# Products of the conditioning vector with the modulations' weights: from VectorE multiply-adds to float32 matmuls in quarters of the TensorE array, and the first stage's weights loaded in rows of 2 KB

## The chip, the core and the metric

One NeuronCore of a Trainium2 chip runs the whole program. Its engines work through queues of their own, each in order: TensorE (PE: matmuls, float32 and a faster one-pass form called fp32r), VectorE (DVE), ScalarE (ACT), GpSimd (POOL) and SyncE (SP), which here issues nearly all DMAs. They meet through semaphores. The metric is the device time of one execution in microseconds; lower is better.

## The reference

One decoder block over 1024 tokens of 1024 channels. A conditioning vector `c` gives six modulation vectors of 1024 channels each; they shift, scale and gate what goes into and comes out of two sublayers. The change touches only how `mod` is computed, and how the weights of `u` (the first 512 columns of `w_in`) are loaded:

```python
cond = jax.nn.silu(c)
mod = (cond @ w_ada[l] + b_ada[l])[:, None, :]        # w_ada: 1024 x 6144
sh1, sc1, g1, sh2, sc2, g2 = jnp.split(mod, N_ADA, axis=-1)
h = modulate(rmsnorm(x, norm1_g[l]), sh1, sc1)        # x (1 + sc1) + sh1
proj = h @ w_in[l]
u, q, k, v, gate_a, gate_b = jnp.split(proj, IN_SPLITS, axis=-1)
y_a = s5_branch(u, ...) @ w_a[l]                      # a state-space scan, then a gated unit w_glu
y_b = stick_breaking_attention(q, k, v) @ w_b[l]
merged = (jax.nn.sigmoid(gate_a) * y_a + jax.nn.sigmoid(gate_b) * y_b) @ w_o[l]
x = x + g1 * merged                                    # then a feed-forward part with sh2, sc2, g2
```

All is float32.

## The kernel before

The code is Python that records instructions; a scheduler then orders them on each engine by a simulated timeline, within the data dependencies and the turns of the buffers, and tiles are handed out in the order in which the program asks for them. A tile whose buffer is still in use makes its first writer wait, and a pool that is closed gives its memory to the next pool, whose first writers wait for all that used it.

*The opening, `start` (from L507).* The 1024 x 1024 input is loaded in two halves of four row tiles; each half is normalised and transposed by TensorE into `xT`. The vector is held as `cond[p, k] = silu(c)[8p + k]`. For each of eight blocks of 128 channels, `ada(k)` loads the shift and the scale columns of `w_ada` into a tile `wa` (two DMAs in rows of 512 bytes, three buffers), VectorE forms `acc`, a sum over `k` of `wa[:, k] * cond[:, k]`, in one multiply (L555) and seven multiply-adds (L559), and a matmul with a column of ones (L563) adds up the 128 partitions. Then `modulate(k, 0)` writes the channels of the first half as two fp32r terms, high (ScalarE, L571) and low (VectorE L572, GpSimd L573), and `product` (L582) adds them into the four `u` results. The weights of `u` come in four blocks of 128 columns, all 1024 rows of each, in rows of 512 bytes, and are split into high and low as well. The second half of the input follows when five blocks are done.

*The S5 stage.* From the end of the opening the state-space branch (class `S5`) runs in four rounds: `tables(m)`, a long run of small GpSimd operations (L67 to L72), then `run(m)` with loads of `u`, TensorE products (L287, L325, L326) and VectorE scans. Between its parts TensorE works off the value projection (`v_proj`, L639) and the first eight gates (`gate`, L619); gates 6 and 7 may load their weights only after the last S5 product. The results of `v_proj` and of the gates take turns in two PSUM buffers, `mm` of the pools `mm` and `mg`.

*`ada_rest` (L753 to L765)* belongs to the same stage. It forms the other four modulation vectors, 4096 columns of `w_ada`, in eight pieces of 512 columns: four loads `aw` of two `k` each (512 KB, rows of 2 KB, two buffers), eight VectorE operations into `acc` (L762, L764), and a store to `aD` in DRAM. `aD` is read back much later, for the merge and the feed-forward part, where the 128 partitions are added up.

*After it, `glu` (from L801)* reads the S5 result back from DRAM (`raw`, L810), applies GELU (L811), splits it into `yp` and multiplies it with `w_glu` (TensorE, tiles `ga`). Its tiles lie in the memory that the S5 stage gives back. The query and key projections and the attention follow.

Of the kernel before, what the change touches and what calls it, by code (L numbers as in the profile page):

```python
# [9 lines left out]
F32 = mybir.dt.float32  # L10
# [327 lines left out]
AK = 2  # L338

GAB = 4  # L340
TPB, WAB = 2, 3
# [5 lines left out]
XH1 = 5  # L347
# [37 lines left out]
class Block:  # L385
# [121 lines left out]
    def start(self, const, up):  # L507
# [4 lines left out]
        w_v = i["w_ada"].rearrange("o (p k) (s n) -> (o p) k s n", k=KT, n=1024)  # L512
        self.hT = [[pool.tile([P, 2, 512], F32R, name=n) for _ in range(KT)] for pool, n in ((self.PA, "pa"), (self.PB, "pb"))]
        with self.pool("s0", 1, side="right") as sp, self.pool("s0a", 1, side="right") as ap, \
# [6 lines left out]
            ws, chain = [], []  # L521
# [26 lines left out]
            def ada(k):  # L548
                w = ap.tile([P, KT, 2, P], F32, name="wa", bufs=WAB)
                for q in range(2):  # L550
                    self.last_ada = nc.sync.dma_start(out=w[:, :, q], in_=w_v[:, :, q, P * k:P * k + P])
                if k < 4:
                    ws.append(self.u_weight(k, ring=None if k < 3 else (up, "u3h", "u3l", self.wring[0][3], "ws", 2)))
                acc = ap.tile([P, 2, P], F32, name="acc", bufs=2)
                ins = nc.vector.tensor_scalar(acc, w[:, 0], self.cond[:, 0:1], None, ALU.mult)  # L555
                if chain:
                    self.after(ins, chain[-1])
                for j in range(1, KT):
                    ins = nc.vector.scalar_tensor_tensor(acc, w[:, j], self.cond[:, j:j + 1], acc, ALU.mult, ALU.add)  # L559
                chain.append(ins)  # L560
                for q in range(2):
                    o = ps[:, q, k:k + 1]
                    nc.tensor.matmul(o, lhsT=acc[:, q], rhs=self.ones[:, 0:1], start=True, stop=True)  # L563
                b = self.cols[:, 64:80].rearrange("p (q k) -> p q k", q=2)
                nc.vector.tensor_tensor(mod[:, :, k], ps[:, :, k], b[:, :, k], ALU.add)
                nc.vector.scalar_tensor_tensor(G[:, k:k + 1], mod[:, 1, k:k + 1], 1.0, self.cols[:, 48 + k:49 + k], ALU.add, ALU.mult)
# [13 lines left out]
            def product(q, m, k, h):  # L580
                for n, (a, b) in enumerate(PRODUCTS):
                    nc.tensor.matmul(q, lhsT=ws[m][a][:, k], rhs=self.hT[h][k][:, b], start=k + n == 0, stop=k + n == KT + 1)  # L582
# [6 lines left out]
            for k in range(KT):  # L589
                ada(k)  # L590
                modulate(k, 0)
                for m in range(min(k + 1, 4)):
# [714 lines left out]
```

## Time and profile before

| what | us |
|---|---|
| median of 3 runs | 1623.77 |
| lowest and highest of them | 1619.41, 1629.88 |
| the profiled execution | 1618.39 |
| its span, first to last instruction | 1616.7 |
| TensorE busy | 1475.8 (91%) |
| VectorE busy | 1106.9 (68%) |
| GpSimd busy | 705.3 (44%) |
| ScalarE busy | 626.6 (39%) |

Busy times are unions over the span, so they say nothing of which engine ends last in a given stage. In rows of the profile `L559` is a line of the kernel, `out<-in` are the program's names of tiles, `x8` is a count, and a bracket holds the idle time ahead of a row with what ended it. Rows of the clock give the share of its full speed that TensorE was granted.

### The profile page before, as it was taken

What the parts mean: (1) busy time and instruction counts of PE and PEld (TensorE: products, weight loads), DVE (VectorE), ACT (ScalarE), POOL (GpSimd) and SP (SyncE); (2) the same over time, 40 slices, a digit from 0 to 9 for tenths busy, and PEclk for the clock granted to TensorE, in tenths of its full rate; (3) what the DMA queues carried; (4) which work ended last, traced back from release to release, by engine and by line L of the source; (5) the groups of instructions that cost most, each with busy time, mean ns of one, the idle gap of its engine ahead of it and who ended that gap; (6) DMA issues with size and microseconds to landing.
All of it is one profiled execution on the core that took longest, in us unless ns stands there. A gap on an engine that the chain in (4) does not pass through costs nothing.

```text
span 1616.7 us, 18487 instructions
## 1 busy us (share of the span) xinstructions
PE 1475.8 (91%) x6738; PEld 1153.8 (71%) x6738; DVE 1106.9 (68%) x1399; ACT 626.6 (39%) x816; POOL 705.3 (44%) x553
## 2 busy tenths in 40 slices
PE   4888897999989899999999979999999998999965
PEld 3688676787645476665778758888888886887854
DVE  6989887342475645545743788666566659999978
ACT  4421111532575745535423643332323334443313
POOL 3559784010110102110340454445555458788784
PEclk9999999899899999999999989999999999999988
DMA  9585665627101012111742323333333146445302
GB/s 241 164 205 171 167 184 159 181 85 221 46 0 40 27 46 85 53 46 46 242 175 91 109 74 111 98 99 113 114 114 117 65 155 249 147 159 163 98 26 104
DMA packets 191139, 193.55 MB, mean 120 GB/s; under 512 B 28069, under 2 KB 141833, under 8 KB 191049
## 3 DMA queue, kind: packets, MB, share of 16 engines
q1 hardware_dynamic: 179976, 184.38, 36.9%
q10 hardware_dynamic: 11072, 8.00, 1.7%
q8 instruction: 53, 0.87, 0.2%
q14 instruction: 38, 0.30, 0.1%
HBM read 142.40 MB, written 48.76 MB: 118 GB/s over the span
## 4 chain that ended last, share of the span: by engine, by line
PE 49%; DVE 21%; issue 9%; POOL 8%; DMA 8%; ACT 5%; SPq 1%; ACTq 0%; DVEq 0%; POOLq 0%
PE mm L619 11%; PE tq L1031 10%; PE wo L1031 8%; PE wo L912 5%; PE ga L619 3%; PE gu L1031 3%; PE z L699 2%; DVE acc L559 2%; PE mm L746 2%; DMA aw<-in_w_ada_dram 2%; PE acc L736 2%; PE acc L741 1%; DVE acc L764 1%; DVE x L1119 1%; POOL pb L1123 1%
## 5 line engine op out<-in xcount | busy, mean ns | idle before, releaser
L430 POOL TENSOR_TENSOR ws<-wb 128x1024 f32<-128x1024 f32 x29 | 73.2, 2526 | 102.9 <-DVE wl L433 59.5
L738 DVE TENSOR_TENSOR wa<-wa,acc 128x512 f32<-128x512 f32 (+3 forms) x96 | 52.9, 552 | 87.5 <-PE acc L736 87.0
L414 POOL TENSOR_TENSOR wl<-ws,wh 128x1024 fp32r<-128x1024 f32 x10 | 25.4, 2544 | 192.7 <-ACT wh L411 192.7
L413 POOL TENSOR_SCALAR wgh<-wgs 128x1024 fp32r<-128x1024 f32 x8 | 8.7, 1092 | 206.8 <-PE mm L619 146.1
L430 POOL TENSOR_TENSOR wgs<-wb 128x1024 f32<-128x1024 f32 x15 | 37.0, 2466 | 107.3 <-DVE x L433 36.1
L743 ACT ACTIVATE wa<-wa 128x1024 f32<-128x1024 f32 (+3 forms) x48 | 40.4, 842 | 67.8 <-DVE wa L738 67.6
L1084 POOL TENSOR_TENSOR pa<-pa,row 128x1024 f32<-128x1024 f32 x22 | 64.4, 2950 | 2.1 <-DMA pa<-in_w_ffn_down_dram 2.1
L714 DVE COPY wa<-z 128x1024 f32<-128x1024 f32 (+1 forms) x40 | 44.6, 1116 | 29.1 <-ACT ws L713 18.0
L619 PE MATMUL mm<-pa,wh 128*128 128x512 f32 x192 | 63.9, 410 | 0.0
L1022 POOL TENSOR_TENSOR f<-f,f 128x512 f32<-128x512 f32 x30 | 50.1, 1694 | 26.8 <-DVE f L1012 18.3
L619 PE MATMUL mm<-pb,wh 128*128 128x512 f32 x192 | 60.4, 395 | 0.8 <-DVE k L673 0.8
L717 DVE SCALAR_TENSOR_TENSOR ws<-wa,ws 128x1024 f32<-128x1024 f32 (+1 forms) x40 | 48.2, 1208 | 16.9 <-ACT ws L716 16.7
L619 PE MATMUL mm<-pa,wgh 128*128 128x512 f32 x176 | 56.5, 402 | 1.3 <-POOL wgh L413 0.9
L619 PE MATMUL mm<-pb,wgh 128*128 128x512 f32 x176 | 57.4, 406 | 0.2 <-ACT gst L656 0.2
L411 ACT CAST wh<-ws 128x1024 fp32r<-128x1024 f32 x30 | 31.4, 1046 | 63.8 <-PE wo L912 27.6
L764 DVE SCALAR_TENSOR_TENSOR acc<-aw,cond,acc 128x512 f32<-128x512 f32 x56 | 46.9, 837 | 12.2 <-DMA aw<-in_w_ada_dram 11.7
L719 DVE TENSOR_TENSOR wl<-ws,wh 128x1024 fp32r<-128x1024 f32 (+1 forms) x40 | 46.0, 1150 | 13.0 <-ACT wh L718 12.3
L699 PE MATMUL z<-q,k 64*128 64x512 f32 (+3 forms) x192 | 48.3, 574 | 4.8 <-DVE wa L714 2.9
L713 ACT ACTIVATE ws<-z 128x1024 f32<-128x1024 f32 (+1 forms) x40 | 37.4, 936 | 33.6 <-DVE wl L719 32.4
L718 ACT CAST wh<-ws 128x1024 fp32r<-128x1024 f32 (+1 forms) x40 | 38.3, 957 | 28.9 <-PE acc L741 22.5
L1011 ACT ACTIVATE f<-f 128x1024 f32<-128x1024 f32 x22 | 23.4, 1061 | 62.3 <-DVE f L1051 32.5
L1104 POOL TENSOR_TENSOR wb<-pa 128x512 f32<-128x512 f32 x23 | 40.6, 1775 | 15.7 <-DVE wxl L1102 5.5
(736 smaller groups left out, 4892.5 us busy)
## 6 DMA issues: line engine op xcount, KB each, us to landing
aw<-in_w_ada_dram SPq DMA_DIRECT2D x32, 512.0 KB, 5.2
hD<-f SPq DMA_DIRECT2D x30, 512.0 KB, 3.4
wb<-in_w_ffn_gate_dram SPq DMA_DIRECT2D x44, 256.0 KB, 4.0
wb<-in_w_ffn_up_dram SPq DMA_DIRECT2D x44, 256.0 KB, 4.5
pa<-in_w_ffn_down_dram SPq DMA_DIRECT2D x22, 512.0 KB, 6.3
wb<-hD SPq DMA_DIRECT2D x40, 256.0 KB, 2.8
ws<-in_w_in_dram SPq DMA_DIRECT2D x19, 512.0 KB, 6.5
x<-in_x_dram SPq DMA_DIRECT2D x16, 512.0 KB, 7.1
```

The source lines that it names most:

```text
L430: (add or nc.gpsimd).tensor_tensor(st, a, b, op)
L619: self.nc.tensor.matmul(ps, lhsT=w[a][:, k], rhs=act[h][k][:, b], start=(j == 0), stop=(j == n - 1))
L699: ins = nc.tensor.matmul(z[:, x, f:f + w], lhsT=k[h, P * kb:P * kb + P], rhs=q[h, 512 * Q + c:512 * Q + 512], start=f == 0, stop=not diag)
L714: nc.vector.tensor_copy(at, z)
L717: nc.vector.scalar_tensor_tensor(st, at, 0.0, st, ALU.max, ALU.add)
L719: nc.vector.tensor_tensor(lt, st, ht.bitcast(F32), ALU.subtract)
L738: nc.vector.tensor_tensor(a[:, x, f], a[:, x, f], acc[:, x, c], ALU.subtract)
L764: nc.vector.scalar_tensor_tensor(acc, w[:, j], cj, acc, ALU.mult, ALU.add)
L912: nc.tensor.matmul(ps, lhsT=mg[t // 4][k][:, a, P * (t % 4):P * (t % 4) + P], rhs=ws[k // 2][b][:, k % 2], start=(j == 0), stop=(j == 23))
L1022: nc.gpsimd.tensor_tensor(o, a, b, op)
L1031: self.nc.tensor.matmul(ps, lhsT=w[x][:, q, k], rhs=self.B[i](y, k), start=(j == 0), stop=(j == 11))
L1084: nc.gpsimd.tensor_tensor(w, w, g2, ALU.mult)
```

## The change

Both places form the products by TensorE. The vector is widened once to `cond32`, 32 equal columns of `cond[:, k] / 32` for each `k`. `ada_mm` multiplies a piece of 512 columns of `w_ada` with the 32 columns of one `k` and writes 32 PSUM partitions, the quarter `k % 4` of the array; `k` and `k + 4` add up in one quarter. The 128 partitions of the result then again sum to the wanted product, so what follows it is unchanged. The matmuls are plain float32. ScalarE copies the result into `acc`.

In the opening the eight steps become two groups of four channel blocks. Each loads shift and scale columns in four DMAs of 1 MB, in rows of 2 KB, into four buffers. The transposes and these results share the PSUM pool `tp` of two buffers. The weights of `u` now come in four blocks of two `k` and all 512 columns, in rows of 2 KB. The second half of the input is loaded behind group 1's loads.

In `ada_rest` the loads stay as they are, but the result takes one of the PSUM buffers `mm` that `v_proj` and the gates take their turns in.

```diff
 KT = 8
 MASKED = -1.0e30
 
-AK = 2
+AK, ARB = 2, 2
 
 GAB = 4
-TPB, WAB = 2, 3
+TPB, WAB = 2, 4
 GUB, WOB, TQB = 1, 3, 4
 ZPB = 2
 GB = 2
 WAB2, WSB, WHB = 4, 2, 2
 
-XH1 = 5
 QPIN = -10
 PINS = (0, 5, 10, 15, 20, 25, 30, 35)
 
...
         nc, i = self.nc, self.i
         ss = const.tile([P, KT], F32, name="ss1")
         x_v = i["x"].rearrange("o (t p) d -> p (o t) d", p=P)
-        w_v = i["w_ada"].rearrange("o (p k) (s n) -> (o p) k s n", k=KT, n=1024)
+        w_v = i["w_ada"].rearrange("o (p k) n -> (o p) k n", k=KT)
+        self.cond32 = up.tile([P, KT, 32], F32, name="cond32")
+        nc.vector.tensor_scalar(self.cond32, self.cond.unsqueeze(2).broadcast_to([P, KT, 32]), 1.0 / 32.0, None, ALU.mult)
         self.hT = [[pool.tile([P, 2, 512], F32R, name=n) for _ in range(KT)] for pool, n in ((self.PA, "pa"), (self.PB, "pb"))]
         with self.pool("s0", 1, side="right") as sp, self.pool("s0a", 1, side="right") as ap, \
                 self.pool("s0p", 1, PSUM) as pp, self.pool("s0t", TPB, PSUM) as tp, self.pool("s0m", 5 - TPB, PSUM) as mp:
...
             ps = pp.tile([P, 2, KT], F32, name="adap")
             mod = const.tile([P, 2, KT], F32, name="mod1")
             G = const.tile([P, KT], F32, name="G1")
-            ws, chain = [], []
+            ws = []
 
             def half(h):
                 r = self.rstd(const, ss[:, 4 * h:4 * h + 4], 4)
...
                     sq = xT[:, 2 * (t % 4):2 * (t % 4) + 2, 512:1024]
                     nc.scalar.activation(sq, x[t].rearrange("p (a b) -> p a b", a=2), AF.Square, accum_out=ss[:, t:t + 1])
 
-            def ada(k):
-                w = ap.tile([P, KT, 2, P], F32, name="wa", bufs=WAB)
+            def ada(g):
+
                 for q in range(2):
-                    self.last_ada = nc.sync.dma_start(out=w[:, :, q], in_=w_v[:, :, q, P * k:P * k + P])
-                if k < 4:
-                    ws.append(self.u_weight(k, ring=None if k < 3 else (up, "u3h", "u3l", self.wring[0][3], "ws", 2)))
-                acc = ap.tile([P, 2, P], F32, name="acc", bufs=2)
-                ins = nc.vector.tensor_scalar(acc, w[:, 0], self.cond[:, 0:1], None, ALU.mult)
-                if chain:
-                    self.after(ins, chain[-1])
-                for j in range(1, KT):
-                    ins = nc.vector.scalar_tensor_tensor(acc, w[:, j], self.cond[:, j:j + 1], acc, ALU.mult, ALU.add)
-                chain.append(ins)
-                for q in range(2):
-                    o = ps[:, q, k:k + 1]
-                    nc.tensor.matmul(o, lhsT=acc[:, q], rhs=self.ones[:, 0:1], start=True, stop=True)
+                    parts = []
+                    for a in range(2):
+                        w = ap.tile([P, 4, 512], F32, name="wa", bufs=WAB)
+                        n = 2 * q + g
+                        self.last_ada = nc.sync.dma_start(out=w, in_=w_v[:, 4 * a:4 * a + 4, 512 * n:512 * n + 512])
+                        parts.append(w)
+                    t = tp.tile([P, 512], F32, name="tp")
+                    for k in range(KT):
+                        self.ada_mm(t, k, parts[k // 4][:, k % 4])
+                    acc = ap.tile([P, 512], F32, name="acc", bufs=2)
+                    nc.scalar.copy(acc, t)
+                    for k in range(4):
+                        nc.tensor.matmul(ps[:, q, 4 * g + k:4 * g + k + 1], lhsT=acc[:, P * k:P * k + P], rhs=self.ones[:, 0:1], start=True, stop=True)
+                for a in (2 * g, 2 * g + 1):
+                    ws.append(self.u_weight(a, ring=None if a < 3 else (up, "u3h", "u3l", self.wring[0][3], "ws", 2)))
+                s = slice(4 * g, 4 * g + 4)
                 b = self.cols[:, 64:80].rearrange("p (q k) -> p q k", q=2)
-                nc.vector.tensor_tensor(mod[:, :, k], ps[:, :, k], b[:, :, k], ALU.add)
-                nc.vector.scalar_tensor_tensor(G[:, k:k + 1], mod[:, 1, k:k + 1], 1.0, self.cols[:, 48 + k:49 + k], ALU.add, ALU.mult)
+                nc.vector.tensor_tensor(mod[:, :, s], ps[:, :, s], b[:, :, s], ALU.add)
+                nc.vector.scalar_tensor_tensor(G[:, s], mod[:, 1, s], 1.0, self.cols[:, 48 + 4 * g:52 + 4 * g], ALU.add, ALU.mult)
 
             def modulate(k, h):
                 t = self.hT[h][k]
...
 
             def product(q, m, k, h):
                 for n, (a, b) in enumerate(PRODUCTS):
-                    nc.tensor.matmul(q, lhsT=ws[m][a][:, k], rhs=self.hT[h][k][:, b], start=k + n == 0, stop=k + n == KT + 1)
+                    nc.tensor.matmul(q, lhsT=ws[k // 2][a][:, k % 2, P * m:P * m + P], rhs=self.hT[h][k][:, b], start=k + n == 0, stop=k + n == KT + 1)
 
             def store(m, h, q):
                 u = up.tile([P, 8, 64], F32, name="us", bufs=3)
                 self.upin = nc.scalar.copy(u, q.rearrange("p (c j) -> p j c", j=8))
                 nc.sync.dma_start(out=self.uD[P * m:P * m + P, :, 64 * h:64 * h + 64], in_=u)
 
-            for k in range(KT):
-                ada(k)
-                modulate(k, 0)
-                for m in range(min(k + 1, 4)):
-                    for kk in range(k if m < k else 0, k + 1):
-                        product(acc[m], m, kk, 0)
-                if k == XH1:
+            for g in range(2):
+                ada(g)
+                if g:
                     load(1)
+                for k in range(4 * g, 4 * g + 4):
+                    modulate(k, 0)
+                    for m in range(4):
+                        product(acc[m], m, k, 0)
             for m in range(4):
                 store(m, 0, acc[m])
             half(1)
...
     def w3(self, w, n=P):
         return [t.rearrange("p (k n) -> p k n", n=n) for t in w]
 
-    def u_weight(self, m, ring=None):
-        return self.w3(self.weight(self.in_cols(P * m), lo_eng=self.nc.gpsimd, ring=ring))
+    def u_weight(self, a, ring=None):
+        src = self.i["w_in"][0].rearrange("(k p) n -> p k n", p=P)[:, 2 * a:2 * a + 2, 0:512]
+        return self.w3(self.weight(src, lo_eng=self.nc.gpsimd, ring=ring), 512)
 
     def v_proj(self, vp):
 
...
             self.split(hi[:, s], lo[:, s], av)
 
 
+    def ada_mm(self, ps, k, w):
+
+        q = slice(32 * (k % 4), 32 * (k % 4) + 32)
+        self.nc.tensor.matmul(ps[q], lhsT=self.cond32[:, k], rhs=w, start=k < 4, stop=k >= 4)
+
     def ada_rest(self, ap, first):
         nc, i = self.nc, self.i
         w_v = i["w_ada"].rearrange("o (p k) n -> (o p) k n", k=KT)
         for n in range(4, 12):
+            ws = []
+            for k in range(0, KT, AK):
+                w = ap.tile([P, AK, 512], F32, name="aw", bufs=ARB)
+                self.after(nc.sync.dma_start(out=w, in_=w_v[:, k:k + AK, 512 * n:512 * n + 512]), first)
+                ws.append(w)
+            ps = self.mm.tile([P, 512], F32, name="mm")
+            for k in range(KT):
+                self.ada_mm(ps, k, ws[k // AK][:, k % AK])
             acc = ap.tile([P, 512], F32, name="acc", bufs=2)
-            for k in range(0, KT, AK):
-                w = ap.tile([P, AK, 512], F32, name="aw", bufs=2)
-                self.after(nc.sync.dma_start(out=w, in_=w_v[:, k:k + AK, 512 * n:512 * n + 512]), first)
-                for j in range(AK):
-                    cj = self.cond[:, k + j:k + j + 1]
-                    if k + j == 0:
-                        nc.vector.tensor_scalar(acc, w[:, j], cj, None, ALU.mult)
-                    else:
-                        nc.vector.scalar_tensor_tensor(acc, w[:, j], cj, acc, ALU.mult, ALU.add)
+            nc.scalar.copy(acc, ps)
             nc.sync.dma_start(out=self.aD[:, n - 4], in_=acc)
 
     def ada_row(self, row, n, tp, pp, tags):
```

The order of the instructions changes with it. First, the opening, on VectorE before (the `wa` multiplies, then the modulation's scale `G` and the scaled input `xT`):

```order
L555 TENSOR_SCALAR acc<-wa,cond 128x256
L559 SCALAR_TENSOR_TENSOR acc<-wa,cond,acc 128x256 x7
L555 TENSOR_SCALAR acc<-wa,cond 128x256
L559 SCALAR_TENSOR_TENSOR acc<-wa,cond,acc 128x256 x3
L565 TENSOR_TENSOR mod_151<-adap,cols 128x2
L559 SCALAR_TENSOR_TENSOR acc<-wa,cond,acc 128x256
L566 SCALAR_TENSOR_TENSOR G_152<-mod_151,cols 128x1
L559 SCALAR_TENSOR_TENSOR acc<-wa,cond,acc 128x256 x2
L572 TENSOR_SCALAR xT<-xT,G_152,mod_151 128x512
```

and on TensorE after (`tp` are transposes and then the new products, `cond_118` is `cond32`, `adap` the sums over partitions, `mm` the `u` products):

```order
L537 MATMUL tp<-ident,x 128x128 x32
L759 MATMUL tp<-wa,cond_118 32x512 x16
L564 MATMUL adap<-ones,acc 128x1 x8
L586 MATMUL mm<-pa,wh 128x512 x4
L759 MATMUL tp<-wa,cond_118 32x512 x8
L586 MATMUL mm<-pa,wh 128x512
L586 MATMUL mm<-pa,wl 128x512
```

The multiply-adds of a block stood between the modulations of the blocks before it; now two sets of eight matmuls stand ahead of the first modulation and a third in the midst of the first products.

Second, the queue of SP at the end of the S5 stage, before (`tz`, `u` and `yD` are S5's, `gD` the gates' stores, `raw` the first loads of `glu`):

```order
L758 DMA aw<-in_w_ada_dram 128x2x512
L657 DMA gD<-gst 128x512 x2
L758 DMA aw<-in_w_ada_dram 128x2x512
L270 DMA tz<-rt 16x8x112
L270 DMA tz<-rt 16x8x80
L270 DMA tz<-rt 16x8x48
L270 DMA tz<-rt 16x8x16
L758 DMA aw<-in_w_ada_dram 128x2x512
L657 DMA gD<-gst 128x512
L765 DMA aD<-acc 128x512
L657 DMA gD<-gst 128x512
L404 DMA ws<-in_w_in_dram 128x8x128
```

and after, from the last gate's store to the first load of `glu`:

```order
L662 DMA gD<-gst 128x512 x2
L768 DMA aw<-in_w_ada_dram 128x2x512 x2
L403 DMA wgs<-in_w_a_dram 128x4x256
L768 DMA aw<-in_w_ada_dram 128x2x512 x2
L775 DMA aD<-acc 128x512
```

Six more pieces follow in the same way, four `aw` loads and one `aD` store at a time, up to this end of the stretch on SP:

```order
L775 DMA aD<-acc 128x512
L768 DMA aw<-in_w_ada_dram 128x2x512 x2
L775 DMA aD<-acc 128x512
L820 DMA raw<-yD 128x512 x8
L403 DMA ws<-in_w_a_dram 128x4x256
```

Before, the last `aw` load stood ahead of gate 6's weights, between S5's own transfers. Now two `aw` loads are issued near the start of the stage and the other 30 stand behind the last gate's store and ahead of all loads of `raw`.

Third, TensorE from the last gate (`mm<-pb,wgh`) to the first product of `glu` (`ga<-yp`), before:

```order
L619 MATMUL mm<-pb,wgh 128x512 x2
L619 MATMUL mm<-pb,wgl 128x512
L619 MATMUL mm<-pb,wgh 128x512 x2
L619 MATMUL mm<-pb,wgl 128x512
L619 MATMUL ga<-yp,wh 128x512 x2
L619 MATMUL ga<-yp,wl 128x512
L619 MATMUL ga<-yp,wh 128x512 x2
```

and after:

```order
L623 MATMUL mm<-pb,wgh 128x512 x2
L623 MATMUL mm<-pb,wgl 128x512
L623 MATMUL mm<-pb,wgh 128x512 x2
L623 MATMUL mm<-pb,wgl 128x512
L759 MATMUL mm<-aw,cond_118 32x512 x64
L623 MATMUL ga<-yp,wh 128x512 x5
L623 MATMUL ga<-yp,wl 128x512
```

Nothing stood between them before; now all 64 products of `ada_rest` do.

## The prediction

> **What bounds the kernel now.** I read the page's totals first, then stretches of time, then the chain of waits inside the two stages that the change touches, then single tiles. The totals say only that TensorE is the busiest engine. The stretches say where it is not the bound (columns: stretch, its length, busy time and instructions of each engine, granted TensorE clock, DMA share, GB/s):
>
> ```profile
> span 1616.7 us, 18487 instructions
> ...
> 15.30:81.00 65.70, 52.57 (x211) 38.24 (x210) 61.25 (x103) 30.10 (x47) 33.71 (x21) 0.95 0.73 196
> ...
> 98.50:311.50 213.00, 184.90 (x1130) 160.67 (x1130) 163.65 (x262) 42.62 (x62) 141.50 (x266) 0.93 0.64 179
> 311.50:337.50 26.00, 23.95 (x99) 19.29 (x98) 15.35 (x19) 18.48 (x25) 2.39 (x1) 0.93 0.32 106
> 337.50:403.00 65.50, 65.31 (x289) 53.75 (x287) 19.15 (x25) 16.14 (x24) 3.21 (x4) 1.00 0.55 169
> ```
>
> From 15.3 to 81 us VectorE is busy for 61.25 of 65.7 us: the opening is bound there. From 98.5 to 311.5 us run the S5 branch, the value projection, eight gates and, on VectorE, the rest of the modulations (`ada_rest`). TensorE is busy for 184.9 of 213 us, VectorE 163.7, GpSimd 141.5. From 337.5 on TensorE has no gap, so a shift of that point is kept. The chain of waits for the opening, and for 98 to 312 us, by line:
>
> ```profile
> by line: DVE acc L559 43.7%; DVE xT L572 10.9%; DMA x<-in_x_dram 7.9%; DMA wa<-in_w_ada_dram 6.7%; DVE acc L555 5.0%; issue 4.6%; DVE G L566 3.3%; DVE x L532 2.8%; PE mm L582 2.1%; ACT pa L571 2.0%; POOL pa L573 1.6%; SPq L542 1.6%; DVE rv
> ```
>
> ```profile
> by line: DMA aw<-in_w_ada_dram 11.9%; DVE acc L764 9.0%; issue 7.1%; DMA u<-uD 5.8%; DVE scr L303 4.4%; DMA raw<-yD 3.5%; DMA ws<-in_w_in_dram 3.0%; POOL scr L71 2.8%; POOL scr L70 2.8%; DVE scr L310 2.7%; POOL p L67 2.6%; POOL p L68 2.6%;
> ```
>
> So the chain puts 48.7% of 81 us (39 us) on the opening's multiply-adds, and 20.9% of 214 us (45 us) on `ada_rest`'s multiply-adds and loads. That is what the change removes or moves. The second stage however is a mesh, not one chain; TensorE's own waits there were for
>
> ```profile
> PE s5a L235 <- POOL scr L71: 9.8, 4, 3.7
> PE mm L639 <- DVE vst L643: 7.3, 4, 2.8
> PE s5a L326 <- DVE h L318: 5.8, 2, 5.4
> PE s5a L325 <- DMA tz<-rt: 3.6, 1, 3.6
> PE s5a L235 <- POOL scr L72: 1.6, 1, 1.6
> ```
>
> (total us, times, longest): 28.1 us, the most that unblocking TensorE can return.
>
> **Term 1, the opening.** Removed from VectorE:
>
> ```profile
> L559 DVE SCALAR_TENSOR_TENSOR acc<-wa,cond,acc 128x256 f32<-128x256 f32 x56 | 39.6, 707 | 1.1
> ...
> L555 DVE TENSOR_SCALAR acc<-wa,cond 128x256 f32<-128x256 f32 x8 | 4.8, 605 | 0.2 <-DMA wa<-in_w_ada_dram 0.2
> ```
>
> 44.4 us. Added are four sets of eight float32 matmuls, priced below at 1.7 us for four at once on a slow clock, so 4 x 3.4 = 14 us, plus four copies on ScalarE (0.58 us each by the first row below). But the 44 us don't all come off. The work was in eight steps, each followed by its modulation and its products; now it is in two groups. Group 0 needs 4 MB before its first modulation, group 1 another 4 MB, whose loads wait for group 0's matmuls to free the four tiles. Counting through the new order: transposes done at about 23 us, two sets to 30, modulations to 39, group 0's products with set three to 48, set four and its columns to 53, then 4 + 8 modulations on GpSimd at 1.44 us each:
>
> ```profile
> 19.84 0.58 ACT L537 COPY xT<-tp 128x512 f32<-128x512 f32 x1 [0.72 <-PE tp L536]
> ...
> 60.62 1.04 PE L536 MATMUL tp<-ident,x 128*128 128x128 f32 x8
> ...
> 52.32 1.44 POOL L573 TENSOR_TENSOR pa<-xT,pa 128x512 fp32r<-128x512 f32 x1 [3.35 <-DVE xT L572]
> ...
> 81.04 0.10 POOL L209 MEMSET tc<- 128x4 f32 x1
> ...
> 98.54 0.28 PE L639 MATMUL mm<-wh,pa 128*128 128x256 f32 x1
> ```
>
> 53 + 1 + 12 x 1.44 = 71 to 72 us, against 81 now for GpSimd's first step of the S5 tables: 9 us. TensorE still owes, from 54 us, 144 products of 0.23 us (24 take 5.44 us in a row quoted under term 4) and 32 transposes (8 take 1.04 us), some 37 to 38 us: 92 against 98.5, or 6 us. I take -9 for the chain that follows. Ends: 0 (TensorE's backlog decides) and -18. The conditioning vector's widening is one small VectorE instruction while the first loads are under way and costs nothing; if the loads were faster it would cost its own 0.3 us. The `w_in` loads in rows of 2 KB move the same bytes; they stand behind the `w_ada` loads and are needed later, so I cost them at nothing (without that cover: the 3 to 4 us of one load).
>
> **Term 2, relief in the S5 stage.** 64 VectorE instructions leave, 56 of them in this row of the page; GpSimd feels them:
>
> ```profile
> L764 DVE SCALAR_TENSOR_TENSOR acc<-aw,cond,acc 128x512 f32<-128x512 f32 x56 | 46.9, 837 | 12.2 <-DMA aw<-in_w_ada_dram 11.7
> ...
> 229.29 0.62 POOL L67 TENSOR_TENSOR p<-tn,wi 128x256 f32<-128x256 f32 x1
> 229.87 1.07 POOL L68 TENSOR_TENSOR p<-tc,wi 128x256 f32<-128x256 f32 x1
> ...
> 229.67 0.79 DVE L764 SCALAR_TENSOR_TENSOR acc<-aw,cond,acc 128x512 f32<-128x512 f32 x1 [1.06 <-DMA aw<-in_w_ada_dram]
> ```
>
> The same GpSimd shape takes 0.62 us alone and 1.07 us across a multiply-add: 0.45 us each. GpSimd is busy for 141.5 of the 185 us to its end in this stage (76%), so 64 x 0.45 x 0.76 = 22 us come off the table chain, which is the one TensorE waits for most. Ends: -5 (the other VectorE work takes the place) and -40 (all 28.1 us of waits and the slow clock behind them). With term 1 the gates end at about 311.5 - 9 - 22 = 280 us. Next late there is TensorE itself: its 184.9 us must then fit between 92 and 280 us, less where its clock rises.
>
> **Term 3, the moved step, is a cost that the diff does not show.** In the new order 30 of the 32 `aw` loads stand on SP behind the last gate's store, and all 64 matmuls on TensorE between the last gate and the first `ga` product of `glu`. (The result tiles come from the same two PSUM buffers as the gates, so they queue behind them.) Before, the loads and multiply-adds lay inside the S5 stage. Only two `aw` buffers exist: each load waits for the matmuls on the load two before it. So there are 15 rounds of issue, landing, two matmuls, with nothing else for TensorE:
>
> ```profile
> L758 SPq DMA_DIRECT2D aw<-in_w_ada_dram x32: 368/386/931, 99.0 to 270.1; - x32
> ...
> DMA to landing us min/median/max: 3.6/5.2/6.4
> ```
>
> ```profile
> 453.65 1.08 PE L746 MATMUL mm<-wa,V 128*64 128x512 f32 x4 [0.77 <-ACT wa L743]
> ...
> 286.75 0.43 PE s5a L325 x2
> ...
> 289.51 0.22 PE s5a L325 x2
> ```
>
> A whole float32 matmul of 128 columns takes 0.22 us, or 0.43 on the slow clock, so one of 512 takes 0.86 or 1.7. The two half-array matmuls of 512 columns above together took 1.08, not 1.7: parts of the array run at once. Quarters were not run before; I take two at once for 1.1 us (full clock) to 1.9 us (slow), and 1.5 as the middle. Landing: 5.2 was among other traffic at some 180 GB/s; here two loads are alone, so nearer the minimum: 4.2. A round is 4.2 + 0.45 + 1.5 = 6.15 us, 15 rounds 92 us. Ends: 3.6 + 0.4 + 1.1 = 5.1, or 76 us; 5.2 + 0.5 + 1.9 = 7.6, or 114 us.
>
> The clock itself is a question: TensorE will be idle for most of each round. The row of 0.43 above comes right after the 5.4 us wait for `h`, the row of 0.22 some 3 us later, so the middle of 1.5 us stands between the two clocks. The Trainium skill, page "TensorE: Matmul & The Clock Gate", section "Loop structure matters more than you think", speaks against this layout: a long wait for a DMA ahead of every matmul lets the array fall back to half its clock. By it a round would be 4.2 + 0.45 + 1.9 and the stretch 98 us, against 86 us at full clock. The trace of before agrees in so far as it shows both clocks on the same instruction.
>
> **Term 4, the lead-in of `glu`.** SP now issues the `raw` loads behind the last `aD` store and waits for it to land, since its buffer lies in memory that is being reused. Now the lead-in lies beside the gates of 290 to 311 us:
>
> ```profile
> 301.67 1.28 ACT L811
> 302.97 2.17 ACT y L811 x2
> ...
> 315.00 1.05 ACT yp L798
> 316.10 21.43 PE ga L619 x86
> 337.53 5.44 PE mm L619 x24
> ...
> aD<-acc SPq DMA_DIRECT2D x8, 256.0 KB, 3.4
> ...
> raw<-yD SPq DMA_DIRECT2D x8, 256.0 KB, 2.7
> ```
>
> Bare: copy and issue 1.1, store 3.4, issue 0.4, `raw` 2.7, GELU 2.2, cast 1.05, so 11 us to the first product; the other three pairs of GELU, cast and load pace the next 13 to 14 us, and the last 14 us are the remaining products: 38 us, against 26 us from gates to 337.5 now. +12, and 1 for the slow clock: +13 (8 to 17).
>
> **Sum.** 1618.4 (the profiled execution; its span is 1616.7) - 9 - 22 + 92 + 13 = 1692. The median of the runs shown lies 5 us above that execution and their spread is 10 us; I give 1695 for a median.
>
> **Rivals.** (a) No change, not slower: the chain's reading is right in full and 39 + 45 = 84 us come off in place of 31. With the short round of 5.1 us: 1618 - 84 + 76 + 13 = 1623. It decides where a round is under (84 - 13) / 15 = 4.7 us; below that the kernel gets faster. For it: the two percentages. Against: GpSimd's 141.5 us and TensorE's 184.9 us remain when VectorE's work is gone. Chance 0.08. (b) Quarters don't run together in float32: two matmuls per round take 3.4 us on the slow clock, a round 8.05, the stretch 121 us: 1618 - 31 + 121 + 13 = 1721. Against it the 1.08 row, in halves only. Chance 0.1. (c) The loads overlap so well that the stretch runs at the DMA's rate; with two of them out it was
>
> ```profile
> GB/s 66 45 125 221 162 57 102 160 98 193 172 82 66 33 98 180 344 262 360 393 377 410 393 393 361 295 410 328 360 393 393 328 377 377 360 342 285 297 279 367
> ```
>
> about 380 GB/s, so 30 x 0.524 MB take 41 us: 1618 - 31 + 41 + 13 = 1641. Against it: each buffer waits for its matmuls, and the fastest landing was 3.6 us. Chance 0.06. (d) The forecast, 0.76.
>
> **Numbers.** A difference under about 1% (16 us) can't be told from none. 1695 is the forecast's. The range: low end, relief -49 with rounds of 5.1: 1618 - 49 + 76 + 8 = 1653, opened to 1647 toward (c); high end, relief -15 with rounds of 7.6: 1618 - 15 + 114 + 17 = 1734, which holds (b). Chances: slower 0.91, same 0.06, faster 0.03.
>
> **What would show it.** Right: a stretch of 76 to 114 us after the last gate with TensorE under 50% busy, its matmuls waiting for `aw`, a period of 5 to 7.6 us; GpSimd's table start near 72 us; the last gate's end near 280; the 64 multiply-adds gone, VectorE some 95 us less busy (44.4 and 46.9 and the eight first products); from the first `ga` product on, the old trace shifted. Wrong: matmuls on `aw` inside the S5 stage, or the gates' end before 250 us, or a stretch of 50 us.

## The result, and the profile after

The changed kernel takes 1698.7 us (median of 4 runs, 1695.5 to 1702.7), the kernel before 1621.6 us in runs of the same time (4 runs, 1619.2 to 1629.9). The ratio is 1.0467, with a 95% interval of 1.0422 to 1.0513. The profiled execution took 1698.87 us, its span is 1696.9 us.

First the totals and the clock row of the page of the changed kernel (the clock row: 40 equal slices of the span, 42 us each, in tenths of full speed):

```profile
span 1696.9 us, 18729 instructions
...
PE 1521.2 (90%) x6930; PEld 1149.6 (68%) x6930; DVE 1021.9 (60%) x1260; ACT 634.2 (37%) x828; POOL 683.5 (40%) x553
...
PEclk9998999558999999999999988999999999999988
```

VectorE lost 85 us, GpSimd 22 us although none of GpSimd's instructions was taken away (553 before and after), and TensorE has 45 us more. The clock row has a hole at slices 7 and 8 (counted from 0), 297 to 382 us. The stretches (length; busy time and instructions of PE, PEld, DVE, ACT and POOL; granted clock, DMA share, GB/s) place it:

```profile
72.00:92.00 20.00, 19.57 (x96) 16.44 (x95) 15.80 (x70) 7.15 (x11) 3.71 (x8) 1.00 0.54 105
92.00:290.40 198.40, 177.55 (x1115) 153.59 (x1118) 120.67 (x205) 33.77 (x54) 120.35 (x266) 0.95 0.37 100
290.40:383.00 92.60, 56.35 (x128) 5.81 (x128) 1.92 (x2) 4.93 (x9) 0.00 (x0) 0.56 0.69 198
383.00:419.50 36.50, 25.48 (x97) 19.60 (x98) 14.88 (x17) 25.60 (x31) 2.40 (x1) 0.80 0.24 80
419.50:485.00 65.50, 65.29 (x289) 53.73 (x287) 19.41 (x25) 16.33 (x25) 3.24 (x4) 1.00 0.55 171
```

The S5 stage, gates included, ends at 290.4 us instead of 311.5. Then come 92.6 us in which TensorE runs nothing but `ada_rest` (128 matmul records: each of the 64 float32 products leaves two), VectorE is busy for 1.9 us, GpSimd not at all, and the clock is 0.56. The lead-in of `glu` follows with 36.5 us, where it was 26. From 419.5 on the last row repeats the old stretch of 65.5 us from 337.5 on: the whole loss lies ahead of it, 419.5 - 337.5 = 82 us, against 80.2 us in the spans.

Inside the 92.6 us, a piece of the chain of waits of the changed kernel (start, length, what), and its end:

```profile
345.68 1.94 PE mm L759 x4
347.64 4.14 DMA aw<-in_w_ada_dram
351.83 1.95 PE mm L759 x4
353.79 3.62 DMA aw<-in_w_ada_dram
357.45 1.95 PE mm L759 x4
...
380.98 1.95 PE mm L759 x4
382.99 0.59 ACT acc L774
383.60 2.01 DMA aD<-acc
385.68 0.34 SPq L820
386.02 0.05 issue
386.07 2.48 DMA raw<-yD
...
406.51 13.00 PE ga L623 x56
```

This is the round that was predicted: a load from its issue to its landing, the two products that read it (x4 records), and only then the next load into the same buffer. The second buffer runs the same cycle half a round later, so a round of some 6 us moves two loads. After the last round follows the predicted chain, copy, store, `raw`, GELU, `ga`.

### The profile page after: what moved, and what is told of

The parts are those of the page before. It is cut to its first block, busy times and chain, and to the rows that moved or that the text cites. A ratio compares the mean times of both kernels' runs of the same rounds, so it can differ in the third digit from the quotient of the medians.

```text
span 1696.9 us, 18729 instructions
## 1 busy us (share of the span) xinstructions
PE 1521.2 (90%) x6930; PEld 1149.6 (68%) x6930; DVE 1021.9 (60%) x1260; ACT 634.2 (37%) x828; POOL 683.5 (40%) x553
## 4 chain that ended last, share of the span: by engine, by line
PE 56%; DVE 15%; DMA 10%; issue 7%; POOL 6%; ACT 5%; SPq 0%; DVEq 0%; ACTq 0%; POOLq 0%
PE mm L623 13%; PE tq L1041 9%; PE wo L1041 7%; PE wo L922 5%; DMA aw<-in_w_ada_dram 4%; PE gu L1041 2%; PE ga L623 2%; PE tq L1123 2%; PE mm L759 2%; PE z L704 2%; PE wo L1123 2%; PE mm L751 2%; PE acc L741 1%; PE mm L586 1%; PE acc L746 1%
## 5 line engine op out<-in xcount | busy, mean ns | idle before, releaser
L759 PE MATMUL mm<-aw,cond 128*32 128x512 f32 x128 | 56.5, 1002 | 36.1 <-DMA aw<-in_w_ada_dram 36.1
L809 DVE TENSOR_TENSOR yp<-y,yp 128x1024 fp32r<-128x1024 f32 x4 | 4.9, 1225 | 109.1 <-ACT yp L808 109.1
L759 PEld LDWEIGHTS mm<-aw,cond 128*32 128x32 f32 x128 | 5.9, 136 | 85.3 <-DMA aw<-in_w_ada_dram 64.6
L704 PE MATMUL z<-q,k 64*128 64x512 f32 (+3 forms) x192 | 44.9, 535 | 8.0 <-DVE wa L719 5.8
```

The costliest lines, as they stand in the source:

```text
L704: ins = nc.tensor.matmul(z[:, x, f:f + w], lhsT=k[h, P * kb:P * kb + P], rhs=q[h, 512 * Q + c:512 * Q + 512], start=f == 0, stop=not diag)
L759: self.nc.tensor.matmul(ps[q], lhsT=self.cond32[:, k], rhs=w, start=k < 4, stop=k >= 4)
```

## The experiments

All ratios below are to the kernel before, on the same chip. The first four take the change apart and then take away what sent `ada_rest` behind the gates.

**The opening alone.** `start` as changed, `ada_rest` as before:

```diff
-            ps = self.mm.tile([P, 512], F32, name="mm")
-            for k in range(KT):
-                self.ada_mm(ps, k, ws[k // AK][:, k % AK])
...
+                        nc.vector.scalar_tensor_tensor(acc, w[:, j], cj, acc, ALU.mult, ALU.add)
```

> The changed opening with the old ada_rest (multiply-adds on VectorE). Theory: the opening is worth the 9.5 us by which the value projection starts earlier in the changed kernel (89.0 against 98.5), and the S5 stage keeps its old length: 1612 us, between 1606 and 1617. Rival, the chain of waits read in full: 39 us off, 1583. Rival, the S5 stage swallows it because GpSimd's tables start only 4.1 us earlier (76.9 against 81.04): 1618 to 1622, no change.

Measured: 1614.6 us, ratio 0.9959 (0.9938 to 0.998), so 3 to 10 us are gained. GpSimd's tables start at 77.9 us. The S5 products (name, number, min/median/max in ns, start of first and last) and the stage's engines, in this kernel:

```profile
L326 PE MATMUL s5a<-h,o x64: 271/275/579, 160.4 to 286.2; 128*128 128x128 f32 x64
...
90.00:309.00 219.00, 182.85 (x1129) 157.93 (x1129) 166.49 (x277) 44.83 (x64) 142.19 (x266) 0.93 0.65 180
...
PE s5a L235 <- POOL scr L71: 17.3, 4, 5.9
```

Before, the last S5 product started at 289.7. It now comes 3.5 us earlier, GpSimd's 266 instructions take 142.2 us as before (141.5). What the opening gives is small: the tables start 3.1 us earlier, and the span is 4.0 us shorter. The time lies in the theory's range, but its mechanism does not hold: the value projection starts 8.6 us earlier (89.9), and TensorE then waits longer for GpSimd's tables, 17.3 us in 4 waits (the last row) in place of 9.8. That is the step that the second rival named, and it swallows about half.

**`ada_rest` alone.** `start` as before (plus the one instruction that makes `cond32`), `ada_rest` as changed. Of this edit against the kernel before, only the added instruction is shown:

```diff
+        self.cond32 = up.tile([P, KT, 32], F32, name="cond32")
+        nc.vector.tensor_scalar(self.cond32, self.cond.unsqueeze(2).broadcast_to([P, KT, 32]), 1.0 / 32.0, None, ALU.mult)
...
```

> The old opening with the new ada_rest (float32 products on TensorE, results in the mm buffers). Theory: the two parts add up, so this is the changed kernel without the opening's 9.5 us: 1708 us, with a stretch of some 92 us of aw rounds behind the last gate. Rival: the shorter S5 stage comes from the opening and not from VectorE's missing multiply-adds; then the last gate ends near 311 as before and the time is 1621.6 + 92 + 11 = 1725.

Measured: 1707.5 us, ratio 1.0516 (1.0498 to 1.0533), 0.5 us from the theory. In this kernel the last S5 product, the stage, and the start of the stretch read:

```profile
L326 PE MATMUL s5a<-h,o x64: 270/275/377, 157.3 to 264.9; 128*128 128x128 f32 x64
...
98.50:296.20 197.70, 180.09 (x1137) 156.82 (x1135) 120.60 (x200) 35.44 (x56) 121.05 (x266) 0.96 0.38 100
...
296.22 1.07 PE L756 MATMUL mm<-aw,cond 128*32 128x512 f32 x8
```

So the relief is real and belongs to the multiply-adds: the same 266 GpSimd instructions take 121 us in place of 141.5, and the S5 branch ends 24.8 us earlier. But the last gate ends at 296.2, only 15.4 us earlier than the 311.6 of before. Behind the last S5 product there are now 31 us of gates in place of 22: TensorE has work left over. The rival falls: it put the last gate near 311 and the time at 1725.

**A PSUM buffer of its own** (a pool `arp` of one buffer, opened beside the others), the call left at its place:

```diff
-            ps = self.mm.tile([P, 512], F32, name="mm")
+            ps = self.arp.tile([P, 512], F32, name="ar")
...
```

> The changed kernel, but the results of ada_rest go to a PSUM buffer of their own and not to the mm buffers whose turns the value projection and the gates take. The code still calls ada_rest last. In the new order 22 of its 64 products stand inside the S5 stage and 42 behind the last gate. Theory: the shared turns were what put all 64 behind the gates, and each round of four products that moves inside saves about its 6 us: 5 rounds of 15 go, 1698.7 - 30 = 1668 us. Rival: the bank alone hides everything: near 1600. Rival: the place does not matter, since loads are issued late in any case: 1699.

Measured: 1676.6 us, ratio 1.0321 (1.0303 to 1.034). The direction is the theory's; 22 us came off where 30 were put. The 42 products behind the gates take this stretch, at the same rate and clock as before:

```profile
295.00:356.00 61.00, 37.55 (x87) 4.24 (x86) 1.92 (x2) 3.97 (x6) 0.00 (x0) 0.55 0.67 198
```

The stretch is 31.6 us shorter, as the theory had it, but it starts 4.6 us later (295.0 for 290.4), with the 22 other products now inside the stage.

**A buffer of its own, and the call ahead of the S5 rounds:**

```diff
+                        self.ada_rest(ap, self.upin)
                         for m in range(4):
                             s5.run(m, s5.tables(m), self.uD[P * m:P * m + P], self.yD[P * m:P * m + P])
...
-                        self.ada_rest(ap, self.upin)
```

> As own_bank, with ada_rest called ahead of the S5 rounds, so that the order puts all 64 products inside the S5 stage, mostly two at a time. Theory: the stretch of 92.6 us behind the gates and the longer lead-in (10.6) go, and the products cost TensorE at most 32 pairs x 1.0 us there, of which part falls into its 21 us of idle time: 1698.7 - 103 + 10 = 1606 us (1596 to 1620), with the last gate ending between 290 and 310. That would be faster than the kernel before (1621.6) by about 1%. Rival: a pair that waits for its load holds all of TensorE's queue behind it, some 2 us for each of 32 loads: 1698.7 - 103 + 64 = 1660.

Measured: 1613.7 us, ratio 0.9929 (0.9905 to 0.9954): 0.5 to 1% under the kernel before, and 85 us below the changed kernel, with the same products on the same engine. The stretch is gone; the late place in the order and the buffer turns together were its cause. The early call with the shared buffers was not run. Of this kernel, the group of the products, the S5 products and the stage:

```profile
L759 PE MATMUL ar<-aw,cond 128*32 128x512 f32 x128 | 33.2, 605 | 0.1
...
L326 PE MATMUL s5a<-h,o x64: 271/275/377, 149.7 to 271.4; 128*128 128x128 f32 x64
...
90.00:309.00 219.00, 209.15 (x1256) 157.68 (x1257) 132.54 (x215) 54.22 (x78) 118.42 (x266) 0.98 0.65 184
...
308.65 0.39 PE L623 MATMUL mm<-pb,wgl 128*128 128x512 f32 x1
```

S5 ends 18 us earlier than before, yet the last gate ends at 309, 2.6 us earlier. TensorE is busy for 209 of 219 us: it has become the bound of this stage, and the 33.2 us of products on it use up what VectorE and GpSimd gave back. Its gain over the kernel with the opening alone can't be told from nothing by these runs: the two intervals overlap.

**Four at once.** As the last one, with the order of the products fixed, so that the four of two loads stand together:

```diff
-            for k in range(KT):
-                self.ada_mm(ps, k, ws[k // AK][:, k % AK])
+            prev = None
+            for k in (2, 3, 0, 1, 6, 7, 4, 5):
+                ins = self.ada_mm(ps, k, ws[k // AK][:, k % AK])
+                if prev is not None:
+                    self.after(ins, prev)
+                prev = ins
```

> As own_bank_called_first, but the order of the products is fixed so that the four on two loads stand next to each other, the one on the later load first. Theory: in own_bank_called_first TensorE itself was the bound (33.2 us of products, in pairs, moved its last gate to 308.9 though the last S5 product had come to 271.3); four quarters at once take as long as two, so some 16 us come off TensorE: the last gate ends near 293 and the time is 1613.7 - 15 = 1598 (1593 to 1606). Rival: TensorE was not the bound there, or four at once take twice as long as two: 1610 to 1616, no change. Rival: holding the products for the later load blocks TensorE's queue: above 1620.

Measured: 1623.0 us, ratio 1.0013 (0.9997 to 1.0029). The time was missed by 25 us. The same rows of this kernel, with TensorE's wait for GpSimd's tables (total us, times, longest):

```profile
L759 PE MATMUL ar<-aw,cond 128*32 128x512 f32 x128 | 19.3, 663 | 0.1
...
90.00:309.00 219.00, 200.15 (x1272) 158.68 (x1272) 129.89 (x217) 57.51 (x81) 118.99 (x266) 0.96 0.65 185
...
PE s5a L235 <- POOL scr L71: 11.6, 4, 3.9
```

Four at once do cost less, 19.3 us for 33.2. But of those 13.9 us only 2.8 reach the first query product of the attention part, which starts at 327.8 for 330.6: TensorE now waits 11.6 us for GpSimd's tables, where it waited 1.8. And from that product to the end this kernel takes 1294.1 us, where the other kernels of this study take 1277 to 1283. The scheduler, which places work by a simulated timeline, had also changed the order of the attention's matmuls behind it; that this costs the 11 us or more is likely, but not shown. So the total says nothing of the products here, and the stage's own times have to be read.

**Half on VectorE.** As the one called first, with the odd pieces on VectorE:

```diff
+            if n % 2:
+                for k in range(KT):
+                    wk, ck = ws[k // AK][:, k % AK], self.cond[:, k:k + 1]
...
+                        nc.vector.scalar_tensor_tensor(acc, wk, ck, acc, ALU.mult, ALU.add)
+            else:
```

> As own_bank_called_first, but four of the eight pieces of ada_rest (the odd ones) are again multiply-adds of VectorE. Theory: half of the 33.2 us leave TensorE, half of the relief of VectorE and GpSimd is given up (last S5 product some 7 us later, 278); the last gate ends 8 to 15 us earlier than 308.9: 1613.7 - 10 = 1604 (1599 to 1609). Rival: with VectorE back in the stage the S5 chain decides again: 1612 to 1616.

Measured: 1621.9 us, ratio 1.0006 (0.9988 to 1.0024). Both theories missed, the rival by less. The last S5 product starts at 288.9, no earlier than with all the work on VectorE (286.2), though GpSimd's 266 instructions take 131.3 us, about half way between 141.5 and 118.4. TensorE waits for GpSimd's tables nearly as long as with all the work on VectorE (17.3 us in opening_only), where it was 1.8 us with none of it:

```profile
PE s5a L235 <- POOL scr L71: 16.4, 4, 6.2
```

Half the work away is not half the relief; why the tables come as late as with all of it was not followed further.

**Called between the value projection and the gates, with the shared buffers:**

```diff
+                        self.ada_rest(ap, self.upin)
                         for m in range(KT):
                             self.gate(0, m, gp, s5.last_mm if m >= 6 else None)
-                        self.ada_rest(ap, self.upin)
```

> The changed kernel (results of ada_rest in the shared mm buffers), but ada_rest is called between the value projection and the gates. In the new order its 64 products stand ahead of nearly all gates, among the last S5 rounds. Theory: the place alone removes most of the stretch, since the gates then fill TensorE behind it, but with shared buffers TensorE waits for the loads while the gates stand behind: S5 ends near 255, the eight gates (384 matmuls of 0.23 us, 87 us) follow, the last ends near 340 and the time is 1699 - 55 = 1645 us (1625 to 1665), between the changed kernel and the one with a buffer of its own (1614). Rival: only a buffer of its own helps: 1690 or above. Rival: the place is all: 1614.

Measured: 1689.6 us, ratio 1.0444 (1.039 to 1.0497): 45 us above the theory, and where the first rival put it (1690). TensorE's waits from 150 to 292 us and the stage, in this kernel:

```profile
PE mm L759 <- DMA aw<-in_w_ada_dram: 22.3, 14, 7.1
PE s5a L325 <- DMA tz<-rt: 19.2, 3, 9.3
...
90.00:309.00 219.00, 151.98 (x934) 106.82 (x935) 115.94 (x196) 28.14 (x49) 116.42 (x266) 0.79 0.51 141
```

S5 ends at 256, but TensorE is busy for only 152 of 219 us. The gates, which used to fill its gaps, must wait for their turn behind `ada_rest` in the two buffers: the first of their products starts at 286.7 and the last ends at 385. So this earlier place alone brings little. With the shared turns it is now the gates that come late.

The other four look into a round of the stretch.

**Both products of a load in one quarter:**

```diff
-                self.ada_mm(ps, k, ws[k // AK][:, k % AK])
+                q = slice(32 * (k // 2), 32 * (k // 2) + 32)
+                nc.tensor.matmul(ps[q], lhsT=self.cond32[:, k], rhs=ws[k // AK][:, k % AK], start=k % 2 == 0, stop=k % 2 == 1)
```

> The changed kernel, but in ada_rest the two products on one load go to the same quarter of the array (quarter k // 2, where k and k + 1 add up), so that they cannot run side by side. Theory: the pair took 1.95 us in the stretch because its two quarters ran at once; one after the other it takes about 3.4 to 3.9 us at the same clock, a round 4.2 + 0.45 + 3.4 = 8.05 us in place of 6.2, and the stretch grows by 15 x 1.5 to 15 x 1.95 = 22 to 29 us: 1721 to 1728. Rival: quarters never ran at once, the 1.95 us are two products in turn: no change, 1699.

Measured: 1703.7 us, ratio 1.0517 (1.0489 to 1.0545), which overlaps the changed kernel's. By the total the rival would hold. The rows say otherwise. TensorE in the changed kernel (start, length, records, and in brackets the idle time ahead):

```profile
342.91 1.92 PE L759 MATMUL mm<-aw,cond 128*32 128x512 f32 x4 [0.82 <-DMA aw<-in_w_ada_dram]
345.68 1.92 PE L759 MATMUL mm<-aw,cond 128*32 128x512 f32 x4 [0.85 <-DMA aw<-in_w_ada_dram]
```

and with one quarter, with the whole stretch:

```profile
343.16 1.90 PE L773 MATMUL mm<-aw,cond 128*32 128x512 f32 x4 [1.14 <-DMA aw<-in_w_ada_dram]
345.91 1.90 PE L773 MATMUL mm<-aw,cond 128*32 128x512 f32 x4 [0.85 <-DMA aw<-in_w_ada_dram]
...
291.00:385.70 94.70, 61.97 (x129) 11.81 (x128) 1.92 (x2) 5.08 (x8) 0.00 (x0) 0.93 0.65 194
```

A pair takes 1.9 us in both, but here the granted clock is 0.93, and 0.56 there. In one quarter two products go one after the other at nearly full clock; in two quarters they go together at half of it. My theory was right on the quarters and wrong to keep the clock fixed.

**Fewer waits.** Six matmuls that nobody reads behind each pair, in a fixed order:

```diff
+                if k % AK == AK - 1:
+                    for j in range(6):
+                        ins = nc.tensor.matmul(warm, lhsT=self.ident_r, rhs=self.hT[0][0][:, 0], start=j == 0, stop=j == 5)
...
```

> The changed kernel, with six fp32r matmuls of 512 columns, whose result nobody reads, behind each pair of products of ada_rest, so that TensorE waits less. Theory: the half clock of the stretch (granted 0.56) comes from TensorE's idle share there; filled, it is granted nearly the full clock, a pair takes 1.07 us in place of 1.92, six matmuls 1.4 us, both fit into the 2.85 us between two loads, and a round is 4.2 + 0.45 + 1.07 = 5.7 us: the stretch 86 us in place of 92.6, 1692 us. Rival: two quarters at once are held at half clock whatever the idle share; then a pair and six matmuls take 1.92 + 2.7 = 4.6 us for each of 30 loads, the stretch 138 us: 1744.

Measured: 1691.9 us, ratio 1.0449 (1.0413 to 1.0484). The rival (1744) falls by the total. The theory's 1692 is met, but the interval overlaps that of the changed kernel, so that anything was gained can only be read from the rows:

```profile
336.76 1.05 PE L759 MATMUL mm<-aw,cond 128*32 128x512 f32 x4 [0.28 <-DMA aw<-in_w_ada_dram]
337.74 1.66 PE L779 MATMUL ar<-pa,ident_r 128*128 128x512 f32 x6
339.33 1.05 PE L759 MATMUL mm<-aw,cond 128*32 128x512 f32 x4
...
289.50:376.40 86.90, 81.52 (x316) 37.21 (x315) 1.92 (x2) 5.08 (x8) 0.00 (x0) 1.00 0.73 212
```

The clock is 1.00, the pair takes 1.05 us in place of 1.92, and from first product to last it is 86.9 us in place of 92.6. Added work that fills idle time made the stretch 5.7 us shorter.

**Two loads for all.** All 64 products read the first two loads (30 loads are left out):

```diff
-                w = ap.tile([P, AK, 512], F32, name="aw", bufs=ARB)
-                self.after(nc.sync.dma_start(out=w, in_=w_v[:, k:k + AK, 512 * n:512 * n + 512]), first)
-                ws.append(w)
+                if len(two) < 2:
+                    w = ap.tile([P, AK, 512], F32, name="aw", bufs=ARB)
+                    self.after(nc.sync.dma_start(out=w, in_=w_v[:, k:k + AK, 512 * n:512 * n + 512]), first)
+                    two.append(w)
+                ws.append(two[k // AK % 2])
```

> The changed kernel without 30 of the 32 loads of ada_rest: all 64 products read the two pieces of weights that the first two loads bring, so the modulations are not the reference's. Theory: the stretch is the landing of loads and hardly the products; what is left is 64 products without waits, 16 sets of four at 1.07 us = 17 us if four quarters run at once, 34 us if only two do, in place of 92.6: 1698.7 - 59 to 76 = 1623 to 1640, the nearer to 1623 the better the four run together. Rival: the copies and stores of the eight results bound the stretch: 8 x (0.6 + 2.5 + 1) = 33 us or more, 1640 or above, with waits for aD.

Measured: 1625.0 us, ratio 1.0018 (1.0001 to 1.0036). The whole stretch of this kernel:

```profile
290.44 7.07 PE L759 MATMUL mm<-aw,cond 128*32 128x512 f32 x64
298.24 7.08 PE L759 MATMUL mm<-aw,cond 128*32 128x512 f32 x64 [0.73 <-ACT acc L777]
```

All 64 products take 14.2 us, 0.88 us for four, at a granted clock of 1.00: four quarters do run at once. The copies of the results hold TensorE up once, for 0.73 us, so the rival falls. Some 78 of the 92.6 us were waits for loads (and the clock that goes with them).

**Half the size, twice the buffers:**

```diff
-AK, ARB = 2, 2
+AK, ARB = 1, 4
```

> The changed kernel, with the weights of ada_rest loaded by one k (256 KB) into four buffers in place of two k (512 KB) into two; the memory and the bytes under way are the same. Theory: the round is the landing of a load and its products, and a load of half the size lands sooner (256 KB: 2.5 to 2.7 us in the lead-in, 512 KB: 3.8): a buffer's cycle is 2.7 + 0.45 + 1.0 = 4.2 us for four loads of 256 KB in place of 6.2 us for two of 512 KB, the stretch 15 x 4.2 = 63 us, 1698.7 - 30 = 1669 us. Rival: the landing is set by the bytes under way, not by the size of one load: 16 rounds of 6 us as before, 1699.

Measured: 1682.8 us, ratio 1.039 (1.0355 to 1.0424): 16 us off, half of what was expected. Its stretch, and the landing of its loads, in the trace of this kernel:

```profile
287.20:363.90 76.70, 56.30 (x129) 8.89 (x128) 1.92 (x2) 4.99 (x8) 0.00 (x0) 0.91 0.77 240
...
DMA to landing us min/median/max: 2.6/3.5/5.1
```

The median landing is 3.5 us, against 3.8 for loads of twice the size: four under way at once hardly land sooner than two. The stretch lies about half way between theory and rival (76.7 us, between 63 and 92.6). The Trainium skill, page "SBUF — State Buffer", section "The DMA setup-cost knee", advises the largest single transfer that one can make, for transfers that the DMA bounds. This stretch, whose buffers wait for products too, went the other way for a given memory: 240 GB/s for 198. A likely reason, not shown apart from the others, is that a buffer is free again after one product and not after two.

## Why the prediction was right

- **Term 3, the moved step (+92):** right in place and mechanism, and 92.6 us in size. That the size came out to 1 us is luck: inside a round two errors cancelled. Issue and landing together were put at 4.65 us and took 3.5 to 5.3 in the chain, 4.06 on average over its 15 rounds; the pair was put at 1.5 and took 1.95, at half clock nearly throughout. So the half clock that was weighed there came, and the stretch still stayed under the 98 us put for it, as the loads landed sooner. The shared buffers and the late call are the cause (own_bank, own_bank_called_first), the loads its length (two_loads).
- **Term 1, the opening (-9):** the value projection starts at 89.0 for 98.5, but GpSimd's tables at 76.9 for 81.04, 4.1 us earlier and not 9. Alone the opening is worth 3 to 10 us by its ratio, and 4.0 by the spans; the gates end only 2.3 us earlier with it. The term was too large.
- **Term 2, the relief (-22):** right for GpSimd itself, which is busy for 120 us in place of 141.5. The step that failed is the one behind it, "the gates end at about 311.5 - 9 - 22 = 280": they end at 290.4, so 21 us came off where 31 were put. It took GpSimd's relief in full for time at the gates' end, and added the two terms. Alone the relief moved the gates' end by 15.4 us (rest_only). What TensorE waited for most in this stage of the changed kernel:

```profile
PE s5a L235 <- POOL scr L71: 8.9, 3, 3.7
PE mm L644 <- ACT vst L648: 5.0, 1, 5.0
PE s5a L325 <- DMA tz<-rt: 3.9, 1, 3.9
```

  The waits for the tables fell from 11.4 (L71 and L72) to 8.9 us only, and the earlier opening lengthens them: 6.6 without it (L71 in rest_only), and 17.3 for 9.8 with the old `ada_rest` (opening_only). From the start of the value projection on, all of TensorE's waits fell from 28.1 to 21.3 us, most of it the wait for `h`, and its busy time from 184.9 to 180.1. With the start 9.5 us earlier, that makes up the 21 us.
- **Term 4, the lead-in (+13):** 36.5 us against 26, so 10.5. Somewhat too large, in the predicted order.
- The sum was 1692, and the profiled execution took 1698.87: 10 us of opening and relief are missing, the lead-in is 2.5 us shorter, and the part from 419.5 on ran 1.8 us shorter than before. The errors partly offset one another.
- **Signs.** The stretch, its waits for `aw` and a period of some 6 us came as named. TensorE was busy for 61% of the stretch and not for under 50%, as the pair took longer at half clock; VectorE lost 85 us and not 95.
- **Rivals.** (a), the chain's reading in full, fell: 84 us were to come off ahead of the stretch, and 21 did; its short round of 5.1 us did not come either. (b) fell: quarters run together. Its price was wrong too, since in one quarter the clock rises and pays for most of it (94.7 us, not 121). (c) fell: the loads ran at 198 GB/s, not 380.

## What to carry to other kernels

When work moves to another engine, look at which buffers its results take turns in: a result tile drawn from a shared ring is placed where the ring is, whatever the data allow, and with two load buffers that place costs a full landing per round. Giving it a free PSUM bank of its own and asking for it early took no further work and saved 85 us. Count the receiving engine's time in the stage first: here TensorE had 21 us idle of 198 in the changed kernel, and with 33 us of products in that stage no gain over the opening alone could be shown.

## What was not expected of the hardware

The clock was not set by the length of the waits alone. In the changed kernel's stretch the 29 waits for loads take 36.1 us, 1.2 on average, and the clock is 0.56; in same_quarter 28 waits take 32.7 us, again 1.2 on average, and the clock is 0.93. Nor does the busy share of the time tell them apart, 61% and 65%. What differs is the work, counted at full clock: 1.05 us of it per 2.9 us, some 36%, against 1.9 us, some 65%. Filled to 94%, the clock was 1.00 (warm). That filling the idle time lifts the clock is shown; that the amount of work decides in same_quarter too is my reading, since there only one quarter at a time was at work as well, and where between 36% and 65% it would turn was not measured.

The Trainium skill, page "TensorE: Matmul & The Clock Gate", section "HAM oscillation — how this bites in real kernels", gives the rule that TensorE must not idle for longer than about 3.4 us at a stretch. The first fall of the clock agrees: it comes with the stretch's longest wait, 4.6 us. But keeping to the rule was not enough here. TensorE's waits in the stretch of the changed kernel (total us, times, longest), and three rows from it:

```profile
PE mm L759 <- DMA aw<-in_w_ada_dram: 36.1, 29, 4.6
...
295.99 3.20 PE L759 MATMUL mm<-aw,cond 128*32 128x512 f32 x8 [4.62 <-DMA aw<-in_w_ada_dram]
...
328.52 1.05 PE L759 MATMUL mm<-aw,cond 128*32 128x512 f32 x4 [2.04 <-DMA aw<-in_w_ada_dram]
331.27 1.92 PE L759 MATMUL mm<-aw,cond 128*32 128x512 f32 x4 [1.70 <-DMA aw<-in_w_ada_dram]
```

From 304 us on no wait is longer than 2.04 us. Yet the clock stays near half, and where it had come back once (the pair of 1.05 us at 328.52) it falls again by the next pair, with waits of 2.04 and 1.70 us around.
